# Row sums of a modulation vector: from GpSimd additions to fused multiply-adds on VectorE, in one float32 layer on one core

## The chip, the core and the metric

The kernel runs on one NeuronCore of one Trainium2 chip. A core has five engines with a queue each, which run their own instructions strictly in order and wait for each other through semaphores: TensorE (PE in the profile, with PEld for its weight loads), VectorE (DVE), ScalarE (ACT), GpSimd (POOL) and SyncE (SP). The metric is the device time of one launch in microseconds (us). The three timed runs of the kernel before took 2408.08, 2408.16 and 2400.03 us; their median is 2408.08.

## What is computed

One layer of a diffusion backbone over 256 latent tokens and 256 context tokens of width 2048, all in float32. A vector `c` gives shifts, scales and gates of two modulated norms. Between the norms stand one wide input projection, two token mixers (RWKV-7 with 16 heads, chunked gated DeltaNet with 8 heads, both in two directions), a gated merge and an output projection; after the second norm comes a SwiGLU feed-forward part.

```python
silu_c = jax.nn.silu(c)[:, None, :]
mod = silu_c @ w_ada[layer] + b_ada[layer]                 # (1, 6 * 2048)
sh1, sc1, gt1, sh2, sc2, gt2 = jnp.split(mod, 6, axis=-1)
h = modulate(rmsnorm(x, norm1_w[layer]), sh1, sc1)
y, yc = mix_tokens(h, hc, ...)
x = x + gt1 * y
x = x + gt2 * swiglu(modulate(rmsnorm(x, norm2_w[layer]), sh2, sc2), ...)
return rmsnorm(x, final_norm_w)
```

The part that matters here is `silu_c @ w_ada` for `gt1`, `sh2` and `sc2`: 6144 columns, a matrix of 2048 x 6144 floats (50 MB) that is read once and multiplied with one vector. The kernel calls it `ada_rest`.

## The kernel before

Everything is transposed: channels on the 128 partitions, tokens along the free axis. A float32 product is made of three TensorE products, since each weight tile is split into a rounded part `whi` (ScalarE, a cast of the raw tile `wraw`) and the rest `wlo` (VectorE, `wraw` minus `whi`). So each 128x512 piece of a weight costs one ScalarE and one VectorE instruction, and then twelve matmuls into a PSUM tile `mm`.

The stages follow each other: the first modulation and the low-rank products; a long middle part in which the RWKV mixer, the DeltaNet mixer and the input projection run side by side; then the merge (weights `pa`, `pb`), the output projection (`wout`) and the feed-forward part (`wgu`, `wdn`).

The middle part is woven by the program itself. Each piece of work is a Python generator that yields instructions for a lane (an engine); the class `Weave` keeps a model time for each engine and always records the instruction that can start first in that model, and of those that can start at the same time the one with the lowest rank. The result is a fixed order on PE, DVE, ACT and POOL, which the chip then follows. Splits of weights have rank -1, the heads of the mixers 0 to 180, `ada_rest` 500 and the input projection's products 900, which fill what TensorE has left. In the profile all these instructions carry line 142, the recording helper, so groups are told apart by their tiles: `arena` holds the mixers' intermediate tiles, `s`, `pa`, `pi` and `mm` are PSUM tiles, `Vn`, `St`, `LT`, `Qe`, `T` and `Tx` belong to the DeltaNet heads.

`ada_rest` (lines 1423 to 1459) starts when the last RWKV pair is out and runs beside the eight DeltaNet heads and the rest of the input projection. It goes through six blocks of 1024 columns with 16 row tiles `w` of 128x1024 each (512 KB, tile `aw`, three buffers in turn):

- GpSimd issues the load of a row tile, as soon as the sum that used its buffer three tiles earlier is made (`"added", i - 3`);
- ScalarE multiplies it in place with `ck[:, k, 0:1]`, the vector's element of each partition (one 128x1024 instruction);
- GpSimd adds it to the block's sum `acc` (one 128x1024 instruction); the first tile of a block is written to `acc` by ScalarE itself.

After 16 tiles, a ones product on TensorE sums `acc` over the partitions, and four small VectorE instructions put the block into `mod`, which the output projection's residual and the second norm read. GpSimd also has one 128x512 multiplication for each head and direction (`arena<-arena,C`) in this part.

Of the kernel before, what the change touches and what calls it, by code (L numbers as in the profile page):

```python
# [13 lines left out]
AF = mybir.ActivationFunctionType  # L14
ALU = mybir.AluOpType
# [252 lines left out]
def emit(ctx: ExitStack, tc, A, out, dbg=None):  # L268
# [6 lines left out]
    e, v, s = Lane(E, 0.027, 0.00083, 0.0), Lane(V, 0.07 * LAT["v"], 0.00104 * LAT["v"], LAT["own"]), Lane(S, 0.06 * LAT["s"], 0.00086 * LAT["s"], LAT["own"])  # L275
    g = Lane(G, 0.06, 0.0024, LAT["own"])
# [18 lines left out]
    def p_(name, i=None, rows=P):  # L295
        lo, hi = _P[name]
        if i is None:
            return PR[:rows, lo:hi]
        return PR[:rows, lo + i:lo + i + 1]
# [97 lines left out]
    ck = cst.tile([P, KT, 2], F32, name="ck")  # L397
# [7 lines left out]
    with tc.tile_pool(name="p0", bufs=1) as p0, \  # L405
# [73 lines left out]
        def low_split(e):  # L479
            res = []  # L480
            for k in range(2):
                pool = p0 if e % 2 else wp
                hi, lo = (pool.tile([P, 8, P] if pool is wp else [P, NL], F32R, tag=f"{t}{k}" if pool is p0 else t, name=t,
                                    bufs=1 if pool is p0 else 2) for t in ("whi", "wlo"))
                if pool is wp:
                    hi, lo = (t.rearrange("p k m -> p (k m)")[:, :NL] for t in (hi, lo))
                S.copy(hi, lws[e][k])
                V.tensor_sub(lo, lws[e][k], hi.bitcast(F32))
                res.append((hi, lo))
            return res  # L490
# [10 lines left out]
        for part in range(NE + 1):  # L501
            if part < NE:
                ps = pst(pmm, "mm")
            for c in range(4):
# [4 lines left out]
                if c == 0 and part < NE:  # L509
                    w = low_split(part)  # L510
# [912 lines left out]
    def ada_rest():  # L1423
        yield ("places",)
        yield "out", NPAIR - 1
        kb = [gs.tile([P, 2, 1024], F32, tag="aw", name="aw") for _ in range(2)]
        acc, ws = kb[0][:, 0], [kb[0][:, 1], kb[1][:, 0], kb[1][:, 1]]
        arow = gs.tile([P, T], F32, tag="arow", name="arow")

        def row_tile(i):  # L1430
            b, k = divmod(i, KT)
            w = ws[i % 3]
            yield g.dma_start(w, A["ada_rest"][b, :, k, :])
            yield 3.5
            if k == 0 and b:
                yield "block", b - 1
            yield s.activation(w if k else acc, w, AF.Identity, scale=ck[:, k, 0:1])
            if k:
                yield "added", i - 1
                yield g.tensor_tensor(acc, w, acc, ALU.add)  # L1440
            weave.ready("added", i)

        for i in range(6 * KT):
            if i > 2:
                yield "added", i - 3
            weave.add(500, row_tile(i))
            if i % KT == KT - 1:
                b = i // KT
                yield "added", i
                ps = yield pab  # L1450
                yield [e.matmul(ps[32 * j:32 * j + 32, 0:T], ones[:, 0:32], acc[:, T * j:T * j + T], start=True, stop=True)
                       for j in range(4)]
                weave.ready("block", b)
                yield v.tensor_copy(arow, ps[:, 0:T])
                yield [e.transpose(ps[:, T + P * q:T + P * q + P], arow[:, P * q:P * q + P], ident) for q in range(2)]
                for q in range(2):
                    o = slice(32 + 8 * b + q, 40 + 8 * b, 2)
                    yield v.tensor_add(mod[:, o], ps[:, T + P * q:T + P * q + P:32], p_("bada")[:, o])
                weave.release(pab)
# [77 lines left out]
    with tc.tile_pool(name="fp", bufs=1, reuse_waits="tile") as fp:  # L1537
# [19 lines left out]
        for j in range(NH):  # L1557
# [6 lines left out]
            g = fp.tile([P, T], F32, tag="g", name="g", bufs=2)  # L1564
# [5 lines left out]
            if 2 <= j < 34:  # L1570

                for a in range(2):
                    c = (j - 2) // 2
                    i = 2 * (j % 2) + a
                    w = fp.tile([P, 512], F32, tag="aw", name="aw", bufs=3)
# [119 lines left out]
```

## Time and profile before

| what | value |
|---|---|
| median of three runs | 2408.08 us (2400.03 to 2408.16) |
| the profiled execution, its own time | 2396.98 us |
| its span (first to last instruction) | 2395.2 us |
| mean granted TensorE clock | 0.974 |
| GpSimd additions `aw<-aw` | 90, first at 846.6 us, last at 1344.8 us |
| loads `aw<-ada_rest` | 96 of 512 KB, first at 837.6 us, last at 1332.8 us |

How such rows are read. In the page, part 1 gives busy time and share of the span, part 2 the span in 40 slices of some 60 us with the busy share in tenths. A row of a group is: line, engine, operation, output<-inputs, shape of output<-input, count, then after the bar the busy time of all in us and the mean duration of one in ns, and after the second bar the time that the engine sat idle just before them and who ended it. A row of the timeline starts with the start in us from the start of the span and the duration in us. A row of the waits is: who waited <- for whom: us in total, times, longest. The view by stretches gives for each stretch its length and each engine's busy time with the count of instructions, the granted clock (1.00 is full speed), the busy share of the DMA engines and GB/s.

### The profile page before, as it was taken

Reading aid. Unit: us, or ns where it says so; the run is one execution under the profiler, and the core shown is the slowest. Engines: PE = TensorE matmul, PEld = TensorE weight load, DVE = VectorE, ACT = ScalarE, POOL = GpSimd, SP = SyncE. Lnnn points to the kernel's source line nnn. Section 1 sums busy time; section 2 is a strip of 40 time slices with the busy share of each in tenths; the row PEclk is TensorE's granted clock in tenths of the full one; section 3 lists DMA queues with packets and bytes.
Section 4 is the critical chain, followed back from the end, with each engine's and each line's share of the span. In section 5 each row is a group of like instructions: output and inputs, shape, how many; then the busy total and the mean of one; then the engine's idle time right before and its main releaser. Section 6 shows DMA issues by size and latency. Waiting matters only on the chain. (4 is left out here: it accounts for less than half of the span.)

```text
span 2395.2 us, 51437 instructions
## 1 busy us (share of the span) xinstructions
PE 2223.7 (93%) x21368; PEld 1946.5 (81%) x21368; DVE 1581.2 (66%) x3057; ACT 1137.9 (48%) x1946; POOL 333.3 (14%) x273
## 2 busy tenths in 40 slices
PE   7989999999999978878778898999999999999998
PEld 4756777777787766766567798989999999999997
DVE  3447688788885587887788754765556556545554
ACT  3255543555445455555445446544444444444443
POOL 0000000000000055575455303000000000000000
PEclk9999999999999989989989899999999999999999
DMA  9946434434433256555445557663777777556665
GB/s 388 381 146 203 149 107 109 108 99 120 115 112 103 87 183 193 160 159 169 138 144 192 175 164 238 205 226 107 232 234 233 235 236 229 189 186 190 192 193 165
DMA packets 232569, 430.57 MB, mean 180 GB/s; under 512 B 114832, under 2 KB 130064, under 8 KB 227984
## 3 DMA queue, kind: packets, MB, share of 16 engines
q1 hardware_dynamic: 204688, 351.78, 46.0%
q0 software_dynamic: 13824, 50.34, 6.2%
q10 hardware_dynamic: 13824, 25.17, 3.3%
q8 instruction: 167, 2.74, 0.5%
q14 instruction: 66, 0.54, 0.1%
HBM read 401.45 MB, written 25.77 MB: 178 GB/s over the span
## 5 line engine op out<-in xcount | busy, mean ns | idle before, releaser
L357 DVE TENSOR_TENSOR wlo<-wraw,whi 128x1024 fp32r<-128x1024 f32 x328 | 393.3, 1199 | 351.6 <-ACT whi L356 349.2
L356 ACT CAST whi<-wraw 128x1024 fp32r<-128x1024 f32 x328 | 337.9, 1031 | 465.3 <-PE mm L367 401.9
L142 PE MATMUL mm<-hxh,wlo 128*128 128x256 f32 (+1 forms) x1376 | 470.1, 342 | 21.6 <-DVE wlo L142 21.2
L142 PE MATMUL mm<-hxh,whi 128*128 128x256 f32 (+1 forms) x1376 | 470.4, 342 | 5.1 <-ACT whi L142 5.1
L142 PE MATMUL mm<-hxl,whi 128*128 128x256 f32 (+1 forms) x1376 | 468.4, 340 | 0.0
L368 PE MATMUL mm<-hfh,wlo 128*128 128x256 f32 x1344 | 375.3, 279 | 0.1
L366 PE MATMUL mm<-hfh,whi 128*128 128x256 f32 x1344 | 374.9, 279 | 0.0
L367 PE MATMUL mm<-hfl,whi 128*128 128x256 f32 x1344 | 374.8, 279 | 0.0
L142 DVE TENSOR_TENSOR wlo<-wraw,whi 128x512 fp32r<-128x512 f32 x344 | 295.5, 862 | 88.3 <-ACT whi L142 86.9
L142 PEld LDWEIGHTS mm<-hxh,wlo 128*128 128x128 f32 x1376 | 266.2, 193 | 53.3 <-DVE wlo L142 26.7
L142 PEld LDWEIGHTS mm<-hxh,whi 128*128 128x128 f32 x1376 | 266.7, 194 | 34.9 <-issue 6.9
L142 PEld LDWEIGHTS mm<-hxl,whi 128*128 128x128 f32 x1376 | 266.3, 194 | 26.8 <-issue 4.7
L142 ACT CAST whi<-wraw 128x512 fp32r<-128x512 f32 x344 | 206.2, 616 | 103.3 <-PE mm L142 80.9
L368 PEld LDWEIGHTS mm<-hfh,wlo 128*128 128x128 f32 x1344 | 252.7, 188 | 0.8 <-DVE wlo L357 0.5
L366 PEld LDWEIGHTS mm<-hfh,whi 128*128 128x128 f32 x1344 | 252.8, 188 | 0.0
L367 PEld LDWEIGHTS mm<-hfl,whi 128*128 128x128 f32 x1344 | 252.7, 188 | 0.0
L142 POOL TENSOR_TENSOR aw<-aw 128x1024 f32<-128x1024 f32 x90 | 218.2, 2424 | 93.3 <-ACT aw L142 89.7
L142 DVE TENSOR_TENSOR arena<-arena 128x28 f32<-128x28 f32 (+13 forms) x538 | 177.6, 332 | 29.3 <-DMA arena<-scr 13.6
L366 PE MATMUL mm<-za,whi 128*128 128x256 f32 x512 | 141.7, 277 | 0.0
L367 PE MATMUL mm<-za,whi 128*128 128x256 f32 x512 | 141.6, 277 | 0.0
L368 PE MATMUL mm<-za,wlo 128*128 128x256 f32 x512 | 141.6, 276 | 0.0
L142 ACT ACTIVATE aw<-aw,ck 128x1024 f32<-128x1024 f32 x96 | 109.6, 1146 | 25.4 <-DMA aw<-ada_rest 24.7
(311 smaller groups left out, 4024.5 us busy)
## 6 DMA issues: line engine op xcount, KB each, us to landing
wraw<-w SPq DMA_DIRECT2D x172, 512.0 KB, 4.1
wraw<-wgu SPq DMA_DIRECT2D x168, 512.0 KB, 4.5
aw<-ada_rest POOLq DMA_DIRECT2D x96, 512.0 KB, 4.1
aw<-ada_first SPq DMA_DIRECT2D x32, 1024.0 KB, 11.7
wraw<-wdn SPq DMA_DIRECT2D x64, 448.0 KB, 3.4
wraw<-wout SPq DMA_DIRECT2D x32, 512.0 KB, 4.4
aw<-ada_gt ACTq DMA_DIRECT2D x64, 256.0 KB, 5.1
wraw<-wdn SPq DMA_DIRECT2D x32, 512.0 KB, 3.5
```

The costliest lines, as they stand in the source:

```text
L142: return Op(self, cost, lambda: getattr(self.engine, name)(out, *a, **k), split)
L356: S.copy(hi[:, c, :M], raw[:, c, :M])
L357: V.tensor_sub(lo[:, c, :M], raw[:, c, :M], hi[:, c, :M].bitcast(F32))
L366: E.matmul(ps, hi, Xh[:, k, :n], start=first and i == 0, stop=False)
L367: E.matmul(ps, hi, Xl[:, k, :n], start=False, stop=False)
L368: E.matmul(ps, lo, Xh[:, k, :n], start=False, stop=last and i == len(wt) - 1)
```

## The change

Each row tile now takes no ScalarE multiplication and no GpSimd addition (except the first of each block). VectorE does both in one instruction, multiply by the partition's scalar and add to `acc`, in place, on halves of 512 columns. The first tile of a block is still scaled into `acc` by ScalarE, now also in halves. The loads are still issued by GpSimd, and `ada_rest` keeps rank 500.

```diff
             yield 3.5
             if k == 0 and b:
                 yield "block", b - 1
-            yield s.activation(w if k else acc, w, AF.Identity, scale=ck[:, k, 0:1])
             if k:
                 yield "added", i - 1
-                yield g.tensor_tensor(acc, w, acc, ALU.add)
+            for n in (0, 512):
+                a = acc[:, n:n + 512]
+                if k:
+                    yield v.scalar_tensor_tensor(a, w[:, n:n + 512], ck[:, k, 0:1], a, ALU.mult, ALU.add)
+                else:
+                    yield s.activation(a, w[:, n:n + 512], AF.Identity, scale=ck[:, 0, 0:1])
             weave.ready("added", i)
```

So 90 GpSimd additions and 96 ScalarE multiplications of 128x1024 go, and 180 VectorE and 12 ScalarE instructions of 128x512 come. The wait for a load moves from ScalarE's queue to VectorE's.

The weaving changes the order on all engines from this place on. On GpSimd, at the start of `ada_rest`, before:

```order
L142 MEMSET TF_9754 128x1024
L142 TENSOR_TENSOR arena<-arena,C 128x512
L123 DMA aw<-ada_rest 128x1024 x4
L142 TENSOR_TENSOR aw<-aw 128x1024
L123 DMA aw<-ada_rest 128x1024
L142 TENSOR_TENSOR aw<-aw 128x1024
```

and now:

```order
L142 MEMSET TF_9754 128x1024
L142 TENSOR_TENSOR arena<-arena,C 128x512
L123 DMA aw<-ada_rest 128x1024 x11
L142 TENSOR_TENSOR arena<-arena,C 128x512
L123 DMA aw<-ada_rest 128x1024 x5
```

The additions are gone; between two of the heads' multiplications GpSimd only issues loads, each of which waits for the sum that frees its buffer.

On VectorE, in the early part of `ada_rest`, where a DeltaNet head's small triangular inverse (`T`, `Tx`) runs, before:

```order
L142 SCALAR_TENSOR_TENSOR arena<-mm,PR,arena 128x254
L142 TENSOR_TENSOR wlo<-wraw,whi 128x512 x2
L142 STREAM_TRANSPOSE Tx<-T_9770 128x256
L142 TENSOR_TENSOR wlo<-wraw,whi 128x512
L142 STREAM_TRANSPOSE T_9770<-Tx 128x256
L142 TENSOR_TENSOR arena<-pi,C 128x128
```

and now, at the same place of the head:

```order
L142 SCALAR_TENSOR_TENSOR aw<-aw,ck 128x512
L142 SCALAR_TENSOR_TENSOR arena<-mm,PR,arena 128x254
L142 SCALAR_TENSOR_TENSOR aw<-aw,ck 128x512
L142 TENSOR_TENSOR wlo<-wraw,whi 128x512
L142 SCALAR_TENSOR_TENSOR aw<-aw,ck 128x512 x2
L142 TENSOR_TENSOR wlo<-wraw,whi 128x512
L142 STREAM_TRANSPOSE Tx<-T_9770 128x256
L142 SCALAR_TENSOR_TENSOR aw<-aw,ck 128x512
L142 STREAM_TRANSPOSE T_9770<-Tx 128x256
L142 SCALAR_TENSOR_TENSOR aw<-aw,ck 128x512
```

The new rows `aw<-aw,ck` stand singly or in twos between the head's and the splits' instructions. The first row shown is the second half of row tile 2 and frees its buffer for row tile 5; the last one shown is the first half of row tile 5 and waits for that load. The eight rows between them are what VectorE has to do meanwhile.

On ScalarE, at the start of `ada_rest`, before:

```order
L142 ACTIVATE aw<-aw,ck 128x1024
L142 CAST whi<-wraw 128x512
L142 ACTIVATE arena<-mm,PR 128x512
L142 ACTIVATE aw<-aw,ck 128x1024 x2
L142 CAST whi<-wraw 128x512 x2
```

and now:

```order
L142 ACTIVATE aw<-aw,ck 128x512 x2
L142 CAST whi<-wraw 128x512
L142 ACTIVATE arena<-mm,PR 128x512
L142 CAST whi<-wraw 128x512 x4
```

ScalarE's casts for the weights now follow each other without the multiplications between them. The last row tile's sum stands at the same distance from the end of the woven part as before: with 306 of the 344 splits `wlo` ahead of the last block's result before, and 302 now. In the feed-forward part, the order on PE is the same as before.

## The prediction

> **What bounds the kernel now.** I read the page first, for where the engines are busy, then the stretches, then the timeline and the groups of the one stretch that the change touches.
>
> ```profile
> span 2395.2 us, 51437 instructions
> ## 1 busy us (share of the span) xinstructions
> PE 2223.7 (93%) x21368; PEld 1946.5 (81%) x21368; DVE 1581.2 (66%) x3057; ACT 1137.9 (48%) x1946; POOL 333.3 (14%) x273
> ## 2 busy tenths in 40 slices
> PE   7989999999999978878778898999999999999998
> ...
> DVE  3447688788885587887788754765556556545554
> ...
> POOL 0000000000000055575455303000000000000000
> PEclk9999999999999989989989899999999999999999
> ```
>
> TensorE is full almost everywhere. It has holes in slices 15 to 22, some 840 to 1380 us, and these are the slices in which GpSimd works and in which the granted clock drops. The chain of waits doesn't reach there: it can be followed back only to this row,
>
> ```profile
> 1340.68 0.14 issue
> ```
>
> so the stage is read by stretches: one before it, the stage itself (the second addition to the last), and what is left of the woven part.
>
> ```profile
> core 0: us, PE busy (x) PEld busy (x) DVE busy (x) ACT busy (x) POOL busy (x), PEclk, DMA share, GB/s
> 280.00:836.00 556.00, 549.92 (x6855) 432.19 (x6854) 433.83 (x1073) 271.03 (x660) 18.11 (x43) 0.99 0.38 106
> 846.00:1347.00 501.00, 404.11 (x3344) 324.50 (x3343) 402.75 (x753) 273.50 (x425) 286.56 (x195) 0.91 0.52 166
> 1347.00:1440.00 93.00, 87.54 (x867) 84.37 (x865) 52.47 (x140) 35.65 (x73) 0.20 (x1) 0.96 0.51 167
> ```
>
> Before the stage, TensorE is busy for 549.9 of 556 us (99%) with VectorE at 78%. In the stage both stand near 80%: TensorE idles for 501.0 - 404.1 = 96.9 us, and its granted clock is 0.91. VectorE's 753 instructions take 402.8 us there, against 433.8 us for 1073 before. That is 535 ns each instead of 404. The timeline shows why. First GpSimd, then VectorE, in the same microseconds:
>
> ```profile
> 846.61 2.36 POOL L142 TENSOR_TENSOR aw<-aw 128x1024 f32<-128x1024 f32 x1 [1.40 <-ACT aw L142]
> 849.27 0.57 POOL L123 DMA_DIRECT2D aw<-ada_rest  x1 [0.30 <-POOL aw L142]
> ```
>
> ```profile
> 846.33 0.20 DVE L142 TENSOR_TENSOR arena<-arena 64x60 f32<-64x60 f32 x1
> 846.46 0.73 DVE L142 SCALAR_TENSOR_TENSOR arena<-mm,PR,arena 128x510 f32<-128x510 f32 x1
> 847.12 1.93 DVE L142 TENSOR_TENSOR arena<-arena 64x60 f32<-64x60 f32 x1
> 848.98 0.73 DVE L142 SCALAR_TENSOR_TENSOR arena<-mm,PR,arena 128x510 f32<-128x510 f32 x1
> ```
>
> A 64x60 product takes 0.20 us when GpSimd is idle. While GpSimd's addition runs (846.61 to 848.97) the same product starts at 847.12 and ends at 849.05, just behind the addition. The 128x510 instruction, which has one input in PSUM (`mm`), takes its 0.73 us under the addition as after it. So a VectorE instruction with both tensors in SBUF stands still until a GpSimd addition ends. VectorE's queue is in order, and what comes behind the blocked instruction waits too:
>
> ```profile
> ACT arena L142 <- DVE arena L142: 45.7, 13, 9.7
> ...
> PEld s L142 <- DVE Vn L142: 32.2, 14, 7.5
> ...
> ACT aw L142 <- DMA aw<-ada_rest: 19.8, 18, 3.0
> ```
>
> ScalarE waits 45.7 us for VectorE's results, the heads' weight loads 32.2 us for `Vn`, and ScalarE itself is held 19.8 us by loads of `ada_rest`.
>
> **The change, part by part.** What the additions cost VectorE is read from groups: the stage, then 1348 to 1440 us, where GpSimd adds nothing.
>
> ```profile
> L142 DVE TENSOR_TENSOR wlo<-wraw,whi 128x512 fp32r<-128x512 f32 x108 | 134.8, 1250 | 29.3 <-ACT whi L142 28.7
> ...
> L142 DVE SCALAR_TENSOR_TENSOR arena<-arena 128x512 f32<-128x512 f32 x7 | 18.0, 2568 | 1.5 <-ACT arena L142 1.4
> L142 DVE TENSOR_TENSOR arena<-arena 64x15 f32<-64x15 f32 x26 | 16.3, 626 | 7.2 <-DMA arena<-scr 6.7
> ...
> L142 DVE TENSOR_TENSOR arena<-arena 64x28 f32<-64x28 f32 x26 | 14.0, 539 | 0.5
> ...
> L142 DVE TENSOR_TENSOR arena<-arena 64x55 f32<-64x55 f32 x26 | 12.7, 487 | 0.5
> ```
>
> ```profile
> L142 DVE TENSOR_TENSOR wlo<-wraw,whi 128x512 fp32r<-128x512 f32 x41 | 27.8, 683 | 15.1 <-ACT whi L142 14.9
> ...
> L142 DVE TENSOR_TENSOR arena<-arena 64x55 f32<-64x55 f32 x4 | 0.8, 201 | 0.0
> ...
> L142 DVE TENSOR_TENSOR arena<-arena 64x28 f32<-64x28 f32 x4 | 0.7, 180 | 0.1
> L142 DVE TENSOR_TENSOR arena<-arena 64x15 f32<-64x15 f32 x4 | 0.7, 167 | 5.5 <-DMA arena<-scr 5.4
> ```
>
> The excess of each group is its count times the difference of the means: `wlo` 108 x (1250 - 683) = 61.2 us; the 128x512 multiply-add 7 x (2568 - 683) = 13.2 (the price without an addition is that of `wlo`, of the same size and also with two SBUF inputs); 64x15 26 x 459 = 11.9; 64x28 26 x 359 = 9.3; 64x55 26 x 286 = 7.4. Sum: 103 us. Groups with a smaller excess are left out, so the sum errs low. GpSimd's tensor work in the stage is
>
> ```profile
> L142 POOL TENSOR_TENSOR aw<-aw 128x1024 f32<-128x1024 f32 x90 | 218.2, 2424 | 93.3 <-ACT aw L142 89.7 <-DVE wlo L142 2.4
> ...
> L142 POOL TENSOR_TENSOR arena<-arena,C 128x512 f32<-128x512 f32 x13 | 18.0, 1387 | 43.5 <-ACT arena L142 43.5
> ```
>
> and only the additions go; the heads' 13 multiplications stay and go on blocking. 218.2 of 236.2 is 92%, so 0.92 x 103 = **95 us of VectorE's time are removed**.
>
> **What is added to VectorE** is 180 multiply-adds of 128x512 with two SBUF inputs. The nearest row is `wlo` at 683 ns; in a queue without gaps the next instruction starts earlier:
>
> ```profile
> 1409.82 0.69 DVE L142 TENSOR_TENSOR wlo<-wraw,whi 128x512 fp32r<-128x512 f32 x1 [3.10 <-ACT whi L142]
> 1410.43 0.42 DVE L142 COPY arena<-pi 128x256 f32<-128x256 f32 x1
> ```
>
> 1410.43 - 1409.82 = 0.61 us. 180 x 0.61 = **110 us are added** (123 at the full 683 ns). VectorE's work in the stage thus goes from 402.8 to 402.8 - 95 + 110 = **418 us**: hardly changed. What changes is where it stands. A blocked instruction costs up to the 2.4 us of an addition, on whatever VectorE's queue has next, often the step a head waits for. A multiply-add costs 0.61 us, and being of rank 500 it stands where the weaving saw VectorE free.
>
> **ScalarE** loses its multiplications (the first row is of the view of tile `aw` and has minimum, median and maximum in ns; the second, from the same view, is for its loads):
>
> ```profile
> L142 ACT ACTIVATE aw<-aw,ck x95: 1132/1148/1166, 845.4 to 1343.4; 128x1024 f32<-128x1024 f32 x95
> ...
> DMA to landing us min/median/max: 3.4/4.1/9.3
> ```
>
> 95 x 1.15 = 109 us of its 273.5 go, and 12 half instructions come back, at most 12 x 1.15 = 14 us. The 19.8 us that its queue stood still for loads go as well. This queue makes `whi`, for which VectorE and then TensorE wait, so some of it is on the path. I don't add it as a term: it is one reason to put VectorE's share below higher than today's 80%.
>
> **The load's wait moves to VectorE.** Behind a waiting multiply-add stand the splits and the heads' steps. In the order shown, the buffer of tile 2 is freed by the first row and needed full by the last. Between them VectorE does nine instructions: six at 0.61 us, two transposes and one 254-wide step, for which I take 0.45 us each from the 256-wide copy's 0.42. That is 5.0 us. A load needs 4.1 us to land, and it starts some 0.4 us after its release (GpSimd waited 60 times, 24.1 us in all, for its own sums before). So the median load is there in time and a late one (9.3 us at worst) isn't. I bound VectorE's waits by nothing and by twice ScalarE's 19.8 us, and take 10.
>
> ```profile
> POOL aw L123 <- POOL aw L142: 24.1, 60, 0.4
> ```
>
> GpSimd's own queue is no danger: its 13 multiplications now stand behind loads, but it loses 218 us of work.
>
> **The sum.** In the new stage VectorE needs 418 + 10 = 428 us and TensorE 404 us at the clock of before. The length lies between 428 (VectorE without a hole) and 501 (nothing gained). TensorE held 99% before the stage with VectorE at 78%; now both are wanted at once, so I take neither: VectorE at 96%, 428 / 0.96 = 446 us, TensorE then at 91%. That is 55 us less. From the profiled execution's own time: 2396.98 - 55 = 2342 us. That execution stood 11 us under the median of the runs and 3 us under the fastest; I add 3 for where a median may fall and forecast **2345 us**.
>
> A rule to be weighed here is the clock. The row has 0.91 in the stage, against 0.99 before it. The Trainium skill, "TensorE: Matmul & The Clock Gate", section "What's actually happening", says that an idle window of about 3.4 us halves TensorE's clock until it has been busy for another. The trace agrees in that the clock falls only where TensorE idles. By the rule TensorE's 404 us would shrink as the holes close (404 x 0.91 / 0.99 = 371 us); by the row alone they stay 404. VectorE's 428 us are the higher floor by both.
>
> **The rivals.** *VectorE is saturated, and nothing is gained.* VectorE's work goes up by 15 us, and its share in the stage stays at 80% because the mixers' chain of steps, not the blocking, leaves the holes: 418 / 0.80 = 522, and with ScalarE's 20 us of waits saved about 500 us. Time 2397 to 2410. For it speaks that the sum is unchanged; against it, that `wlo`, which TensorE's products wait for, alone lost 61 us to blocking, and that VectorE did 78% with TensorE full when nothing blocked it. The Trainium skill, "Perfetto Trace Analysis", section "Optimizing Scalar/DVE Operations", says that GpSimd and VectorE share an SBUF read port, so that moving work between the two might not help; this rival is what that rule would make of the sum, and the blocked 64x60 product agrees with the shared port.
>
> *Loads hold VectorE, and it gets slower.* GpSimd issues a load only after VectorE's sum of three tiles earlier, and VectorE waits in order. If a tile waits 1 us on the mean (90 tiles, 90 us) instead of the 0.1 us that I took, the 55 us are lost and 25 more: 2425 us. It decides from (55 + 12) / 90 = 0.75 us per tile on. Against it stands the 5.0 us of other work in a dense place; for it the landing of up to 9.3 us.
>
> *The blocking falls by more than I counted.* The left-out groups and ScalarE's freedom bring the stage to TensorE's 404 us: 97 us less, 2300.
>
> *The blocking doesn't go:* if GpSimd's issuing of loads, not its additions, blocked VectorE, nothing would go and 110 us of work would come. The row at 849.27 speaks against it: VectorE's 0.73 us step at 848.98 ends on time, but it has a PSUM input. I count this with the slower case.
>
> **How the numbers follow.** The forecast, 12 to 85 us gained, has a chance of 0.70, and the larger gain 0.10. No gain has 0.12. Slower has 0.08. Over 0.5% is 12 us, about what a measurement of this kernel can tell from no change. A gain under 12 us or a loss under 12 us falls to the no-gain case: faster 0.80, same 0.12, slower 0.08. The range runs from the larger gain (2300) to the better end of no gain (2397): it leaves out part of the no-gain case, the slower case and the tail below, some 0.2 in all.
>
> **What would show it.** Right: in the stage, `wlo` near 700 ns instead of 1250, the 64x15 to 64x55 products near their 167 to 201 ns, VectorE's busy time still near 420 us, the stage near 446 us, the granted clock above 0.91, and few and short waits of VectorE for `ada_rest`. Wrong: if `wlo` stays long, if VectorE's waits for loads reach 60 us, or if VectorE runs without a hole and TensorE still idles for 80 us.

## The result, and the profile after

The changed kernel takes 2344.98 us (median of four runs, 2341.4 to 2348.77), against 2408.12 us before (four runs, 2400.03 to 2411.9). The ratio is 0.974, with a 95% interval of 0.971 to 0.977: 63 us, 2.6% faster. A later series on the same chip as other versions gave 2345.36 us and 0.974 (0.971 to 0.978) again.

The page of the profile after, the same rows as shown of before:

```profile
span 2346.7 us, 51488 instructions
## 1 busy us (share of the span) xinstructions
PE 2223.8 (95%) x21368; PEld 1951.7 (83%) x21368; DVE 1557.2 (66%) x3237; ACT 1047.9 (45%) x1863; POOL 113.5 (5%) x183
## 2 busy tenths in 40 slices
PE   7988999999999999999798999999999999999998
...
DVE  3447588778986489889878645765666556545454
...
POOL 0000000000000011111111003000000000000000
PEclk9999999999999999999789999999999999999999
```

TensorE's busy time is the same to 0.1 us (2223.7 before); only the holes in slices 15 to 23 (counted from 1) are smaller. VectorE has 180 instructions more and yet 24 us less busy time.

The stage itself: in this execution everything before it is some 7 us later (GpSimd's multiplication ahead of the first load starts at 843.19 us, before at 836.24), so 846 to 1347 us of before is compared with 853 to 1297 us. The second stretch ends some 15 us behind the last sum and holds fewer matmuls than the first (3210 against 3344); the stage and the rest of the woven part together hold the same (4206 and 4211). Two rows by stretches, the stage and that rest; then the groups of the stage on VectorE.

```profile
853.00:1297.00 444.00, 395.19 (x3210) 323.93 (x3209) 377.87 (x925) 182.04 (x338) 66.80 (x105) 0.93 0.63 187
1297.00:1388.00 91.00, 85.87 (x996) 81.40 (x996) 53.23 (x146) 36.00 (x76) 0.00 (x0) 1.00 0.60 188
```

```profile
L142 DVE SCALAR_TENSOR_TENSOR aw<-aw,ck 128x512 f32<-128x512 f32 x180 | 131.2, 739 | 5.1 <-DMA aw<-ada_rest 4.4 <-ACT aw L142 0.5
L142 DVE TENSOR_TENSOR wlo<-wraw,whi 128x512 fp32r<-128x512 f32 x112 | 78.3, 702 | 6.1 <-ACT whi L142 5.9
...
L142 DVE TENSOR_TENSOR arena<-arena 64x55 f32<-64x55 f32 x26 | 5.2, 202 | 0.3
...
L142 DVE TENSOR_TENSOR arena<-arena 64x28 f32<-64x28 f32 x26 | 4.5, 172 | 0.2
```

The stage takes 444 us instead of 501, and the rest of the woven part 91 us instead of 93: for the same work 535 us instead of 594, 59 us less. The two profiled executions themselves differ by 48 us only (2348.77 against 2396.98), since the one before was faster than all its timed runs and the one after the slowest of its four. Inside the stage `wlo` is back from 1250 to 702 ns, and the small products from 487 and 539 to 202 and 172 ns. VectorE's total falls to 377.9 us although 131.2 us of multiply-adds are in it. What little of the blocking is left comes from the heads' 13 multiplications on GpSimd (experiment 8 shows it).

The waits of the same stretch:

```profile
POOL aw L123 <- DVE aw L142: 145.8, 49, 8.7
...
DVE Tx L142 <- DMA T<-tscr: 20.2, 6, 5.9
ACT arena L142 <- DVE arena L142: 16.8, 7, 4.4
DVE arena L142 <- DMA arena<-scr: 16.6, 5, 7.1
...
PEld s L142 <- DVE Vn L142: 10.3, 13, 3.2
```

The waits behind VectorE are down to a third (45.7 to 16.8 us, 32.2 to 10.3). GpSimd waits 145.8 us before its loads; in this stretch no other engine is found waiting for GpSimd. VectorE now waits 36.8 us for round trips of the heads' inverse through memory (`tscr`, `scr`; 17.2 us before), and 4.4 us for the loads of `ada_rest`.

### The profile page after: what moved, and what is told of

It is laid out like the page before. It is cut to its first block, busy times and chain, and to the rows that moved or that the text cites. A ratio compares the mean times of both kernels' runs of the same rounds, so it can differ in the third digit from the quotient of the medians.

```text
span 2346.7 us, 51488 instructions
## 1 busy us (share of the span) xinstructions
PE 2223.8 (95%) x21368; PEld 1951.7 (83%) x21368; DVE 1557.2 (66%) x3237; ACT 1047.9 (45%) x1863; POOL 113.5 (5%) x183
## 5 line engine op out<-in xcount | busy, mean ns | idle before, releaser
L142 DVE TENSOR_TENSOR wlo<-wraw,whi 128x512 fp32r<-128x512 f32 x344 | 236.2, 690 | 62.7 <-ACT whi L142 60.0
L142 DVE TENSOR_TENSOR arena<-arena 128x28 f32<-128x28 f32 (+13 forms) x538 | 132.0, 247 | 32.1 <-DMA arena<-scr 20.4
L142 DVE SCALAR_TENSOR_TENSOR aw<-aw,ck 128x512 f32<-128x512 f32 x180 | 131.2, 739 | 5.1 <-DMA aw<-ada_rest 4.4
L368 PEld LDWEIGHTS mm<-za,wlo 128*128 128x128 f32 x512 | 96.2, 188 | 0.0
```

What stands on the lines that cost most here:

```text
L142: return Op(self, cost, lambda: getattr(self.engine, name)(out, *a, **k), split)
L368: E.matmul(ps, lo, Xh[:, k, :n], start=False, stop=last and i == len(wt) - 1)
```

## The experiments

The theory (A): a GpSimd addition blocks VectorE's instructions with two SBUF inputs, and the gain is this blocking taken away. The rival (B): the gain comes from ScalarE, which lost 109 us of work and its waits for loads. Ratios are against the kernel before on the same chip, with 95% intervals.

**1. ScalarE's multiplications left out (the sums stay unscaled), GpSimd's additions kept.**

```diff
-            yield s.activation(w if k else acc, w, AF.Identity, scale=ck[:, k, 0:1])
+            if not k:
+                yield s.activation(acc, w, AF.Identity, scale=ck[:, k, 0:1])
             if k:
                 yield "added", i - 1
                 yield g.tensor_tensor(acc, w, acc, ALU.add)
```

> The kernel before without ScalarE's 90 multiplications of row tiles (the sums of the modulation are left unscaled); GpSimd's 90 additions stay. Theory A (GpSimd's additions block VectorE): the blocking stays, wlo in the stage stays near 1250 ns, and only ScalarE's 20 us of waits for loads can go: 2385 to 2410 us. Rival B (ScalarE's freed time made the gain): most of the 63 us come, 2345 to 2370 us, with wlo still long.

Measured: 2427.31 us, ratio 1.008 (1.005 to 1.011). B falls: without ScalarE's multiplications the kernel is not faster but 0.8% slower. The groups of its stage (852 to 1359 us):

```profile
L142 DVE TENSOR_TENSOR wlo<-wraw,whi 128x512 fp32r<-128x512 f32 x101 | 132.9, 1318 | 20.1 <-ACT whi L142 19.9
L142 DVE TENSOR_TENSOR arena<-arena 64x39 f32<-64x39 f32 x26 | 21.9, 843 | 0.7
```

`wlo` is even a little longer than before (1318 against 1250 ns). A foretold the blocking, not the loss, and the time lies outside its range; why it got worse by some 20 us was not tried.

**2. GpSimd's additions left out (no sums are made), ScalarE's multiplications kept, nothing added to VectorE.**

```diff
             yield s.activation(w if k else acc, w, AF.Identity, scale=ck[:, k, 0:1])
-            if k:
-                yield "added", i - 1
-                yield g.tensor_tensor(acc, w, acc, ALU.add)
```

> The kernel before without GpSimd's 90 additions (the sums are left out), ScalarE's 96 multiplications stay, and nothing is added to VectorE. A: wlo near 690 ns, and without the 180 multiply-adds the stage comes nearer to TensorE's 400 us than in the changed kernel: 2300 to 2345 us. B: ScalarE is as loaded as before, no gain: 2395 to 2410 us.

Measured: 2342.42 us, ratio 0.973 (0.970 to 0.976), with `wlo` at 685 ns. Its group (846 to 1274 us), and the loads:

```profile
L142 DVE TENSOR_TENSOR wlo<-wraw,whi 128x512 fp32r<-128x512 f32 x101 | 69.0, 685 | 41.7 <-ACT whi L142 41.3
```

```profile
L123 POOL DMA_DIRECT2D aw<-ada_rest x96: 527/527/722, 835.8 to 1140.3; - x96
```

So the additions' leaving alone gives the whole gain. That it isn't more than with VectorE's sums may have to do with when the loads come: here the last of the 96 is issued 304 us after the first instead of 429 as in the changed kernel (495 before), since ScalarE alone frees the buffers. The next experiment, in which the loads are spread over 427 us again, is 18 us faster; the spread was not tried by itself.

**3. Each GpSimd addition replaced by three memsets of the same tile (no sums are made).** GpSimd is busy for as long as before, writes SBUF and reads nothing.

```diff
                 yield "added", i - 1
-                yield g.tensor_tensor(acc, w, acc, ALU.add)
+                ops = [g.memset(w, 0.0) for _ in range(3)]
+                for o in ops:
+                    o.cost = 0.84
+                yield ops
```

> The kernel before with each GpSimd addition replaced by three memsets of the 128x1024 row tile (about 2.8 us, written to SBUF, nothing read; the sums are left out). A in the form that what blocks is GpSimd's reading of SBUF: wlo near 690 ns and a time as without additions, 2300 to 2350 us. If any GpSimd tensor instruction blocks VectorE: wlo over 1200 ns, 2395 to 2420 us. If GpSimd's own pace (three buffers in turn, each held by the work on it) set the stage: also 2395 to 2420 us, but with wlo short.

Measured: 2324.62 us, ratio 0.965 (0.963 to 0.968). Its stage (849 to 1274 us) by stretches and GpSimd's group, and minimum, median and maximum of `wlo` in it:

```profile
849.00:1274.00 425.00, 383.13 (x3328) 312.57 (x3327) 270.59 (x752) 273.28 (x424) 319.25 (x372) 0.96 0.63 194
```

```profile
L142 POOL MEMSET aw<- 128x1024 f32 x267 | 255.2, 957 | 27.7 <-ACT aw L142 17.4
```

```profile
L142 DVE TENSOR_TENSOR wlo<-wraw,whi x107: 649/683/1249, 851.4 to 1271.4; 128x512 fp32r<-128x512 f32 x107
```

GpSimd is busy for 319 of 425 us, more than before, and VectorE's `wlo` takes 683 ns. So it isn't GpSimd's being busy, its writing or its pace that held VectorE. What the additions do and the memsets don't is read SBUF (and compute on it, which no run takes apart from the reading). This run also gives the stage's floor with no sums on VectorE at all: 425 us, with VectorE at 270.6 us and TensorE at 90%.

**4. The additions in four pieces of 256 columns, still on GpSimd.**

```diff
-                yield g.tensor_tensor(acc, w, acc, ALU.add)
+                for n in range(0, 1024, 256):
+                    yield g.tensor_tensor(acc[:, n:n + 256], w[:, n:n + 256], acc[:, n:n + 256], ALU.add)
```

> The kernel before with each GpSimd addition of 128x1024 in four of 128x256; GpSimd's work stays on GpSimd. If it is the length of the single blockade that costs (up to 2.4 us on one step): wlo under 900 ns and 2350 to 2390 us. If it is the share of time in which GpSimd reads, in whatever pieces: wlo 1200 ns or more and 2400 to 2430 us.

Measured: 2402.84 us, ratio 0.999 (0.997 to 1.001): no difference. VectorE's group in it, from the first load to the last:

```profile
L142 DVE TENSOR_TENSOR wlo<-wraw,whi 128x512 fp32r<-128x512 f32 x130 | 151.8, 1172 | 27.3 <-ACT whi L142 26.9
```

In the kernel before, from the first load to the last:

```profile
L142 DVE TENSOR_TENSOR wlo<-wraw,whi 128x512 fp32r<-128x512 f32 x107 | 129.6, 1213 | 26.5 <-ACT whi L142 25.9
```

So 1172 ns in the mean against 1213. The time is that of the second case of what was expected; its limit for `wlo`, 1200 ns, is just missed. The timeline has the longest case, GpSimd and then VectorE:

```profile
915.61 8.24 POOL L142 TENSOR_TENSOR aw<-aw 128x256 f32<-128x256 f32 x12
923.80 1.61 POOL L123 DMA_DIRECT2D aw<-ada_rest  x3
```

```profile
915.21 9.19 DVE L142 TENSOR_TENSOR wlo<-wraw,whi 128x512 fp32r<-128x512 f32 x1
924.32 0.88 DVE L142 TENSOR_TENSOR arena<-arena 64x39 f32<-64x39 f32 x4
```

Twelve additions run from 915.61 to 923.85; one `wlo` takes 9.19 us and ends at 924.40. VectorE isn't let in between these additions, which follow each other directly. Elsewhere it is, again GpSimd and then VectorE:

```profile
1304.87 7.40 POOL L142 TENSOR_TENSOR aw<-aw 128x256 f32<-128x256 f32 x8 [4.38 <-ACT aw L142]
```

```profile
1308.07 2.21 DVE L142 TENSOR_TENSOR wlo<-wraw,whi 128x512 fp32r<-128x512 f32 x2 [0.57 <-ACT whi L142]
```

These two `wlo` end at 1310.28, 1.99 us before the eight additions do. When VectorE gets in was not found out. What is shown is that pieces of a quarter of the length lower neither the mean of `wlo` by much nor the time. GpSimd also has 55 us more to do with them (388.4 us busy in all against 333.3), so the length of a piece isn't all that differs.

**5. ScalarE multiplies as before, VectorE adds in halves.**

```diff
             yield s.activation(w if k else acc, w, AF.Identity, scale=ck[:, k, 0:1])
             if k:
                 yield "added", i - 1
-                yield g.tensor_tensor(acc, w, acc, ALU.add)
+                for n in (0, 512):
+                    yield v.tensor_tensor(acc[:, n:n + 512], w[:, n:n + 512], acc[:, n:n + 512], ALU.add)
```

> ScalarE multiplies as before, VectorE adds (180 plain additions of 128x512 in place of the multiply-adds); GpSimd only issues loads. A: the blocking goes as in the changed kernel, ScalarE keeps 109 us of work that has room in the stage: 2345 to 2370 us. B: ScalarE is as loaded as before and VectorE gets 110 us more: 2400 us or more.

Measured: 2332.76 us, ratio 0.968 (0.964 to 0.971), 12 us under the lower end of what A foretold. ScalarE's 109 us cost nothing that shows here. Compared with the multiply-add, the plain addition is shorter (rows of tile `aw` in this kernel and in the changed one):

```profile
L142 DVE TENSOR_TENSOR aw<-aw x180: 626/677/1340, 851.5 to 1280.0; 128x512 f32<-128x512 f32 x180
```

```profile
L142 DVE SCALAR_TENSOR_TENSOR aw<-aw,ck x180: 627/735/1227, 855.8 to 1281.2; 128x512 f32<-128x512 f32 x180
```

180 x (735 - 677) = 10 us less for VectorE (9 us in the pages' totals, 1548.5 against 1557.2), about what the run is faster by. The two were not run side by side, and their intervals just touch.

**6. One more multiply-add for each row tile,** into the tile that is done with, so that the result stays the same.

```diff
                     yield v.scalar_tensor_tensor(a, w[:, n:n + 512], ck[:, k, 0:1], a, ALU.mult, ALU.add)
+                    if n:
+                        yield v.scalar_tensor_tensor(w[:, 0:512], w[:, 0:512], ck[:, k, 0:1], a, ALU.mult, ALU.add)
```

> The changed kernel with one more multiply-add of 128x512 for each row tile (90 of them, into the tile that is done with): VectorE gets 90 x 0.73 = 66 us more, 384 + 66 = 450 us in a stage that took 450. If VectorE's share was the bound, as the prediction put it (96% at most): the stage becomes 469 us, 2364 us. If VectorE can only be filled to the 85% that it showed: 529 us, 2424 us. If other waits left the holes and the sums fill them: 2345 to 2355 us.

Measured: 2369.75 us, ratio 0.987 (0.984 to 0.989): 25 us more than the changed kernel, for 60 us more of VectorE (1616.7 us busy in all against 1557.2). Its row from the first load to the last:

```profile
843.00:1374.00 531.00, 468.62 (x3864) 387.97 (x3862) 473.64 (x1133) 206.84 (x393) 69.97 (x109) 0.93 0.60 180
```

The cases "85% at most" (2424) and "other waits only" fall. The time of "VectorE bound at 96%" (2364) is near, but VectorE is busy for 473.6 of 531 us, 89%, where the changed kernel has 85% from its first load to its last. So no case holds as it was put: VectorE can be filled more, at a price of less than half of what is added.

**7. One multiply-add of 128x1024 in place of two halves.**

```diff
-            for n in (0, 512):
-                a = acc[:, n:n + 512]
+            for n in (0,):
+                a = acc[:, n:n + 1024]
                 if k:
-                    yield v.scalar_tensor_tensor(a, w[:, n:n + 512], ck[:, k, 0:1], a, ALU.mult, ALU.add)
+                    yield v.scalar_tensor_tensor(a, w[:, n:n + 1024], ck[:, k, 0:1], a, ALU.mult, ALU.add)
                 else:
-                    yield s.activation(a, w[:, n:n + 512], AF.Identity, scale=ck[:, 0, 0:1])
+                    yield s.activation(a, w[:, n:n + 1024], AF.Identity, scale=ck[:, 0, 0:1])
```

> The changed kernel with one multiply-add of 128x1024 for each row tile instead of two halves: 90 x 1.25 = 113 us of VectorE instead of 180 x 0.73 = 131. If VectorE's busy time counts: 15 us come off its work, 2330 to 2340 us. If what counts is how long a due step stands behind a sum (1.2 us instead of 0.7): 2350 to 2365 us.

Measured beside the changed kernel: 2330.3 us, ratio 0.969 (0.967 to 0.972), against 2345.36 us and 0.974 (0.971 to 0.978). Six runs of it lie between 2324 and 2335 us, six of the changed kernel between 2334 and 2349. Its group, and the row by stretches (853 to 1290 us):

```profile
L142 DVE SCALAR_TENSOR_TENSOR aw<-aw,ck 128x1024 f32<-128x1024 f32 x89 | 114.9, 1290 | 11.9 <-DMA aw<-ada_rest 11.7
```

```profile
853.00:1290.00 437.00, 384.04 (x3328) 313.74 (x3327) 372.32 (x849) 177.61 (x330) 67.93 (x105) 0.95 0.63 190
```

So 15 us less in all, and that a due step can stand 1.3 us behind a sum doesn't show. But VectorE's busy time isn't less by the 16 us that the durations give (180 of 739 ns against 90 of 1290): in the pages' totals it is 7 us, 1550.5 against 1557.2, since each instruction starts a little before the end of the one ahead of it, and there are fewer now. And the weaving gives another order:

```profile
L142 DVE SCALAR_TENSOR_TENSOR aw<-aw,ck x90: 1156/1272/2044, 851.5 to 1188.4; 128x1024 f32<-128x1024 f32 x90
```

The last sum starts at 1188.4 us instead of 1281.2. The gain is measured; whether it comes from VectorE's shorter work or from the order was not tried. With experiment 5 this has the lowest median of the versions that make the sums.

**8. What is left of the blocking, and the wait for loads.** First the heads' multiplications on VectorE too, then 5.0 instead of 3.5 us of model time before each sum, then both, beside the changed kernel.

```diff
-            yield g.tensor_mul(ed, ed, tri[:, d].unsqueeze(1).to_broadcast([P, 4, P]))
+            yield v.tensor_mul(ed, ed, tri[:, d].unsqueeze(1).to_broadcast([P, 4, P]))
...
-            yield 3.5
+            yield 5.0
```

> The changed kernel with the heads' multiplications of 128x512 (16, of which 13 ran in the stage) on VectorE as well, so that GpSimd reads no tensor in the stage. A: what is left of the blocking (wlo 702 ns against 684) goes, and VectorE gets 13 x 0.68 = 9 us more: 2335 to 2350 us, no difference that can be told. If the little blocking that is left still cost as much for each us of GpSimd as the additions did (63 us for 218 us): 5 us faster at most, 2340 us.

> The changed kernel with 5.0 instead of 3.5 us of model time between a load's issue and its sum, so that VectorE's order has more in front of each sum. If loads hold VectorE's queue (the rival of the prediction): 10 us faster or more, under 2335 us. If they don't (VectorE waited 4.4 us in all for them): 2338 to 2352 us.

> The changed kernel once more, beside the two that follow and on the same chip: 2340 to 2350 us, ratio 0.974.

> The heads' multiplications on VectorE and 5.0 us of model time before each sum, together. If each of the two took about 10 us off (2334 us each, not told apart from the changed kernel then) and they add up: 2320 to 2328 us. If what they showed was scatter: 2338 to 2350 us, as the changed kernel beside it.

Measured: in one series 2333.83 us, 0.971 (0.968 to 0.974), for the first, and 2334.33 us, 0.972 (0.968 to 0.976), for the second; in a later one 2345.9 us, 0.976 (0.973 to 0.979), for both, beside 2345.36 us, 0.974 (0.971 to 0.978), for the changed kernel. The first lies 1 us under the range expected, the second 0.7 us inside the case "loads hold VectorE's queue". But the intervals overlap with the changed kernel's, and the two together gain nothing: none can be told from it. `wlo` in the changed kernel (853 to 1297 us) and in the first of these, and VectorE's waits for loads in the second:

```profile
L142 DVE TENSOR_TENSOR wlo<-wraw,whi x112: 623/675/1961, 853.7 to 1296.8; 128x512 fp32r<-128x512 f32 x112
```

```profile
L142 DVE TENSOR_TENSOR wlo<-wraw,whi x109: 629/677/694, 854.4 to 1296.9; 128x512 fp32r<-128x512 f32 x109
```

```profile
DVE aw L142 <- DMA aw<-ada_rest: 5.0, 4, 1.9
```

Without the heads' multiplications on GpSimd the longest `wlo` is 694 ns instead of 1961: they were what was left of the blocking. With later sums VectorE waits 5.0 us for loads instead of 4.4, so the lower median of that run is not a wait for loads taken away. The last 18 us of GpSimd's multiplications, and VectorE's waits for loads, are worth nothing that can be told here.

## Why the prediction was right

The forecast was 2345 us, and 2345 us were measured. The mechanism was that of the runs. That the two numbers agree so closely is luck: two terms of the sum, VectorE's work and its share of the stage, were off by about a tenth each and cancelled each other.

- *A GpSimd addition blocks VectorE's instructions with two SBUF inputs.* Shown: experiment 1 (additions kept, blocking kept), 2 (additions gone, blocking gone) and 3 (GpSimd busy without reading, no blocking). That instructions with one tensor in PSUM aren't held shows in the rows of the same group in the stage, before and after (740 and 732 ns):

```profile
L142 DVE SCALAR_TENSOR_TENSOR arena<-mm,PR,arena 128x510 f32<-128x510 f32 x26 | 19.3, 740 | 0.2
```

```profile
L142 DVE SCALAR_TENSOR_TENSOR arena<-mm,PR,arena 128x510 f32<-128x510 f32 x26 | 19.0, 732 | 0.0
```

- *95 us of VectorE's time are removed.* Too small, as the prediction said of its direction: 402.8 us before against 270.6 us in experiment 3, which has no sums, is 132 us (131 in the pages' totals, 1581.2 and 1449.8). Most of the difference is in groups that were left out of the sum: seven of them, from `arena<-arena` 64x48 (462 ns before, 192 after) to `Qe` (761 and 416), lose another 33 us.
- *110 us are added.* 377.9 - 270.6 = 107 us, and the same in the pages' totals. The mean of one multiply-add is 739 ns, not 683, but as foretold the next instruction starts before its end.
- *VectorE's waits for loads, 10 us.* 4.4 us. The rival in which loads hold VectorE is refuted by that row: its sign was to be 60 us. The loads themselves land later than before (4.7 us in the median against 4.1), but not late enough for the order.
- *The stage, 446 us.* 444 us, and with the rest of the woven part 59 us less where 55 were forecast. VectorE's work and its waits for loads are 382 us instead of 428, and their share 86% instead of 96%. The share was chosen, and it was the weakest step. VectorE isn't the only bound at this load: in experiment 3, with VectorE at 64%, the stage is still 425 us, with TensorE at 90%. So 107 us of sums on VectorE cost 20 us of time (2345.0 against 2324.6), and 60 us more cost 25 (experiment 6). The work near 420 us, which the prediction named as a sign of being right, was 378.
- *ScalarE's relief as a reason for a higher share.* Not shown: with its 109 us kept the time isn't worse, though VectorE then has 9 us less to do (experiment 5).
- *Nothing gained, because a move between two engines that share a port might not help* (the rule of the Trainium skill, "Perfetto Trace Analysis", section "Optimizing Scalar/DVE Operations"). Here the move pays. VectorE's own price for the sums (107 us) is under what GpSimd's additions cost it (132 us). That is 25 us of the 59; that the rest comes from where the instructions stand, the sums in places that the weaving chose and the blocking on whatever came, fits the shorter waits behind VectorE but was not tried by itself.
- *The blocking doesn't go, because GpSimd's issuing of loads is what blocks.* GpSimd still issues all 96 loads, and `wlo` is at 702 ns.
- *The clock.* The granted clock rose from 0.91 to 0.93 in the stage. TensorE's 404.1 and 395.2 us there are not for the same work; for the same work, the stage and the rest, it is 491.7 and 481.1 us, 11 us less, where the prediction's case of a clock without drops was 33 us less in the stage alone. The Trainium skill's rule on idle windows ("TensorE: Matmul & The Clock Gate", section "What's actually happening") agrees with this much, that TensorE still has 444 - 395 = 49 us of holes; nothing was tried on it.
- *The larger gain (2300 us).* Not reached even with no sums at all (2325).

## What to carry to other kernels

When VectorE's mean duration for one and the same shape differs between stretches of a trace, look at GpSimd in the longer one: here its additions held VectorE's instructions with two SBUF inputs, and everything behind them in the queue. Price such GpSimd work by what it costs VectorE (132 us here, for 218 us of additions), not by its own idle engine, and don't count on smaller pieces: a quarter of the length changed nothing here. Compare stretches of two traces only where they hold the same work, and take an engine's gain from its busy time, not from a sum of durations: one sum instead of two halves looked like 16 us less for VectorE and was 7.

## What was not expected

Twelve GpSimd additions of 256 columns in a row held one VectorE instruction for 9.19 us; VectorE wasn't let in between them, though by the records it had started 0.40 us ahead of the first; in another such row of eight it was. And leaving out ScalarE's multiplications made the kernel before slower by 0.8% (0.5 to 1.1): work on an engine with room can space out what collides elsewhere, though that this is the cause was not shown.
